# The output projection by seven products over halves, with branch a merged ahead of branch b

## The chip, the cores and the metric

One core of a Trainium2 chip runs the whole kernel. The metric is device microseconds from launch to end; lower is better. The kernel before took 1390.63 us, the median of 3 runs (1389.96 to 1392.5).

## The reference

One layer over 512 tokens of 2048 channels, all in float32:

```python
h = rmsnorm(x, norm_pre) * (1 + scale) + shift          # shift, scale, gate from c @ w_ada
q_a, f_a, v_a, z_a, v_b, z_b, g_a, g_b = split(h @ w_in)
y_a = hgrn2(q_a, f_a, v_a) / rms * hgrn_norm * silu(z_a)        # gated recurrence, 1024 wide
y_b = pool_mixer(v_b, pool_w, pool_scale) * silu(z_b)           # trailing windows, 1024 wide
merged = sigmoid(g_a) * (y_a @ w_proj_a) + sigmoid(g_b) * (y_b @ w_proj_b)
out = merged @ w_out                                            # 512 x 2048 by 2048 x 2048
return x + gate * rmsnorm(out, norm_post)
```

## The kernel before

Every large product is made of three: each operand is split into a high half that TensorE's fast float32 form holds exactly and the rest (`hi`, `lo`), and hi·hi, hi·lo and lo·hi are summed in PSUM. For weights this is `w_piece` (L156): one load on the sync queue into a `raw` tile, a copy to `hi` on ACT (L162) and the remainder `lo = raw - hi` on DVE, or on POOL where an engine is named or heads are being worked on (L163). `raw`, `whi` and `wlo` have four tiles each, so up to four pieces are under way. `split` (L166) does the same for activations. `load` (L66) fixes the order of the loads, `matmul` (L83) that of the products.

The stages follow each other: norm and modulation of x; the first part of the input projection while h comes in; the rest of it with the recurrence's steps between its products; the two gates g_a and g_b, whose sigmoids stay in SBUF as 32 tiles `sig[b][m]` (L726). Both branches' y have been put into DRAM before (`y_dram`) and are loaded and split again (L731 to L735). Then, for each pair m of 128-channel tiles, branch a's projection (48 products into `pa`), branch b's (48 into `pb`), the two gate products on DVE (L744, L745), their sum (L747) and its split into `mh`, `ml` (L748). Channels are on partitions, tokens along the free axis. TensorE takes the products in the order of the program, from L691 on; the other engines' order comes from a scheduler, which takes the earliest instruction of the program that it holds ready.

The output projection, `out_cols` (L755), has tokens on partitions. For each of four blocks of 512 columns four PSUM tiles are filled, one for a token tile, over 16 k-tiles with three products each:

```python
matmul(outs[t], mh[k][:, sl], w[0][:, r], k == 0, False)
matmul(outs[t], mh[k][:, sl], w[1][:, r], False, False)
matmul(outs[t], ml[k][:, sl], w[0][:, r], False, k == KT - 1)
```

A piece of weights is 2 k-tiles by 512 columns (L766), 24 products. In the last block the second half of the k-tiles goes token tile by token tile, so that a tile is done every 24 products. A done tile is squared and summed on ACT (L778), multiplied by the gate's row on DVE (L780); `finish` (L783) makes 1/rms in small steps on DVE with one square root on ACT, then scales four 512-wide parts and adds x, one part on POOL (L790, L791) and three on DVE (L793), and stores them. x is loaded again on POOL's queue while the last blocks run (L801).

Of the kernel before, what the change touches and what calls it, by code (L numbers as in the profile page):

```python
# [15 lines left out]
P = 128  # L16
D = 2048
S = 512
# [16 lines left out]
def trunk(ctx, tc, x, c, w_ada, b_ada, norm_pre, norm_post, w_in, lower_bounds, hgrn_norm,  # L35
# [4 lines left out]

    const = ctx.enter_context(tc.tile_pool(name="const", bufs=1))
    act = ctx.enter_context(tc.tile_pool(name="act", bufs=1))
    ring = ctx.enter_context(tc.tile_pool(name="ring", bufs=1))
    small = ctx.enter_context(tc.tile_pool(name="small", bufs=2))
# [3 lines left out]

    def t_h(name, dt=F32R):
        return act.tile([P, S], dt, tag="h", bufs=32, name=name)  # L50

    def t_s(name, dt=F32):
        return act.tile([P, S], dt, tag="s", bufs=32, name=name)

    def t_w(name, n=S, dt=F32):
        return act.tile([P, 528], dt, tag="w", bufs=10, name=name)[:, :n]
# [9 lines left out]
    def load(dst, src):  # L66
        """A load on the sync queue, issued in the order of these calls."""
# [15 lines left out]
    def matmul(o, lhsT, rhs, start, stop):  # L83
        """A product; with in_order set, TensorE issues them in the order of these calls."""
        if in_order[0] and last_mm[0] is not None:
            with tc.issue_after(last_mm[0]):
                d = nc.tensor.matmul(o, lhsT, rhs, start=start, stop=stop)  # L87
        else:
            d = nc.tensor.matmul(o, lhsT, rhs, start=start, stop=stop)  # L89
        last_mm[0] = ins_of(d)  # L90
# [5 lines left out]
    # the recurrence's heads, taken in steps between the products of the projections  # L96
# [25 lines left out]
    scan_mask = const.tile([P, S], F32, name="scan_mask")  # L122
    nc.vector.memset(scan_mask, 1.0)
    nc.vector.memset(scan_mask.rearrange("p (c t) -> p c t", t=CH)[:, :, 0:1], 0.0)
    inv_pos = const.tile([P, 16], F32, name="inv_pos")
# [3 lines left out]
    def band_mask(name, step, lo, hi, m, nb):  # L129
        """1 where step * b + lo <= s <= step * b + hi, for column (b, r), r < m."""  # L130
        t = const.tile([P, nb * m], F32, name=name)
# [8 lines left out]
    # masks[m][i][s, t']: s in the i-th quarter of the 4m-block whose later quarters hold t'  # L140
    masks = {m: [band_mask(f"mask_{m}_{i}", 4 * m, i * m, i * m + m - 1, (3 - i) * m, P // (4 * m)) for i in range(3)]
             for m in (2, 8)}
    mask_pair = const.tile([P, P], F32, name="mask_pair")
# [12 lines left out]
    def w_piece(name, src, k0, nk, c0, n, eng=None):  # L156
        """hi and lo halves, exact, of a block of weights: [P, nk, n] each."""
# [28 lines left out]
    # lower bound: softmax over the layers, its running sum less the first layer's  # L186
# [16 lines left out]
    def ada_sum(k, k0, n, src):  # L203
        """Two sums, over the even and the odd row tiles."""
# [11 lines left out]
    def ada(k0, nk, rows=range(KT)):  # L216
        """shift and scale for the k-tiles k0..: the products of c with w_ada, summed over its row tiles."""
        n = 2 * nk * P
        for k in rows:
            a = (t_h(f"ada_{k0}_{k}", F32) if k0 < 4 else t_s(f"ada_{k0}_{k}"))[:, :n]  # L220
# [16 lines left out]
    def rstd_of(ssum, n, tag, r):  # L237
        """r = 1 / sqrt(ssum / n + eps), [P, 1], with one Newton step."""
# [10 lines left out]
    # the scale's share without c: (1 + its bias) * norm_pre  # L249
# [6 lines left out]
    diag = [const.tile([P, P], F32, name=f"diag_{t}") for t in range(TT)]  # L256
# [48 lines left out]
    def cols(name, src, k0, nk, c0, xh, xl, outs, k_first, k_last, eng=None):  # L305
        """128 * len(outs) columns, channels on partitions, over the k-tiles k0.. of a sum k_first..k_last."""
# [29 lines left out]
    def v_half(i):  # L336
        """v for four heads, tokens on partitions."""
# [18 lines left out]
    y_dram = [dram.tile([NH, P, S], F32, name="ya_dram"), dram.tile([NH, P, S], F32, name="yb_dram")]  # L356
    sz_a = [None] * NH
# [397 lines left out]
    def out_cols(j, split_k, done):  # L755
# [11 lines left out]
        for k in range(0, split_k, 2):  # L767
            w = piece(k)
            for t in range(TT):
                for r in range(2):  # L770
                    mm(t, k + r, r, w)
# [60 lines left out]
```

## Time and profile before

| what | value |
|---|---|
| median of 3 runs | 1390.63 us (1389.96 to 1392.5) |
| span of the profiled execution | 1388.9 us |
| busy: PE, DVE, ACT, POOL | 1333.3, 777.2, 521.1, 265.2 us |
| mean granted TensorE clock | 0.990 |
| DRAM read, written | 182.51 MB, 8.39 MB |

The profile gives the span from the first to the last instruction of one execution; the time of that execution itself is not listed apart, and the median of the runs is 1.7 us above the span. Products are pipelined: the duration of one (389 ns) overlaps the next, so their cost is read from the distance of their starts, or from a long link of the chain of waits. [...]

### The profile page before, as it was taken

The page shows a single profiled execution, that of the slowest core. Times are in us where ns is not written, and L with a number is a line of the kernel's source. Part 1 is how long each engine was busy: PE and PEld are TensorE (multiplying, and loading weights), DVE is VectorE, ACT ScalarE, POOL GpSimd, SP SyncE. Part 2 cuts the span into 40 slices and gives each one's busy share as a digit, 9 for nine tenths or more (in the row PEclk, how much of TensorE's full clock was granted, in tenths as well). Part 3 has the DMA queues.
Part 4 walks back from the last instruction along what each step waited for, and adds up shares of the span by engine and source line. Part 5 has one row for each costly group of instructions (what it writes and reads, how often), then busy time and mean ns, then how long its engine had stood idle before and what let it go on. Part 6 is the DMA issues. An engine that isn't in the chain of part 4 may idle for free.

```text
span 1388.9 us, 16351 instructions
## 1 busy us (share of the span) xinstructions
PE 1333.3 (96%) x6105; PEld 1106.5 (80%) x6105; DVE 777.2 (56%) x1237; ACT 521.1 (38%) x745; POOL 265.2 (19%) x273
## 2 busy tenths in 40 slices
PE   2988899999999999999999999999999999999996
PEld 1777788888888888788888888888888888888885
DVE  6996854337668696786834445343254454432326
ACT  5543263353535645465542222222252222221221
POOL 3646451213321332222300000000010000200003
PEclk9999999999999999999999999999999999999999
DMA  9988633322131323323235545554352323623213
GB/s 334 326 291 280 192 110 123 97 84 87 42 129 61 114 76 103 102 73 125 92 119 170 194 146 190 163 179 153 127 167 93 106 91 100 218 92 106 91 61 122
DMA packets 160695, 191.97 MB, mean 138 GB/s; under 512 B 8460, under 2 KB 128356, under 8 KB 160616
## 3 DMA queue, kind: packets, MB, share of 16 engines
q1 hardware_dynamic: 156616, 178.30, 39.2%
q0 software_dynamic: 3840, 12.59, 2.6%
q8 instruction: 48, 0.79, 0.2%
q14 instruction: 31, 0.25, 0.1%
q10 hardware_dynamic: 160, 0.05, 0.0%
HBM read 182.51 MB, written 8.39 MB: 137 GB/s over the span
## 4 chain that ended last, share of the span: by engine, by line
PE 89%; DVE 4%; issue 2%; DMA 2%; POOL 1%; ACT 1%; SPq 0%; DVEq 0%; ACTq 0%; POOLq 0%
PE g_ps L87 25%; PE out L87 11%; PE g L89 7%; PE vb_ps L87 6%; PE za_ps L87 6%; PE v_ps L87 6%; PE pb L87 6%; PE pa L87 6%; PE zb_ps L87 5%; PE q_ps L87 3%; PE lv L87 2%; PE o L87 1%; DVE og L793 1%; DMA x<-in_x_dram 1%; PE mix L87 1%
## 5 line engine op out<-in xcount | busy, mean ns | idle before, releaser
L87 PE MATMUL g_ps<-h_hi,g_hi 128*128 128x512 f32 x512 | 200.5, 392 | 0.0
L87 PE MATMUL g_ps<-h_hi,g_lo 128*128 128x512 f32 x512 | 199.5, 390 | 0.0
L87 PE MATMUL g_ps<-h_lo,g_hi 128*128 128x512 f32 x512 | 199.5, 390 | 0.0
L162 ACT CAST g_hi<-g_raw 128x1024 fp32r<-128x1024 f32 x64 | 67.3, 1053 | 194.8 <-PE g_ps L87 164.1
L163 DVE TENSOR_TENSOR g_lo<-g_raw,g_hi 128x1024 fp32r<-128x1024 f32 x61 | 74.5, 1222 | 107.0 <-ACT g_hi L162 107.0
L87 PEld LDWEIGHTS g_ps<-h_lo,g_hi 128*128 128x128 f32 x512 | 96.4, 188 | 20.1
L87 PEld LDWEIGHTS g_ps<-h_hi,g_hi 128*128 128x128 f32 x512 | 96.4, 188 | 20.0
L87 PEld LDWEIGHTS g_ps<-h_hi,g_lo 128*128 128x128 f32 x512 | 96.3, 188 | 20.1
L211 DVE SCALAR_TENSOR_TENSOR ada_acc<-ada,c_act,ada_acc 128x512 f32<-128x512 f32 (+1 forms) x126 | 105.7, 902 | 0.0
L163 DVE TENSOR_TENSOR wo_lo<-wo_raw,wo_hi 128x1024 fp32r<-128x1024 f32 x32 | 39.2, 1225 | 111.2 <-ACT wo_hi L162 111.2
L87 PE MATMUL out<-wo_hi,m_hi 128*128 128x512 f32 x256 | 99.6, 389 | 0.0
L87 PE MATMUL out<-wo_lo,m_hi 128*128 128x512 f32 x256 | 99.6, 389 | 0.0
L87 PE MATMUL out<-wo_hi,m_lo 128*128 128x512 f32 x256 | 99.6, 389 | 0.0
L162 ACT CAST wo_hi<-wo_raw 128x1024 fp32r<-128x1024 f32 x32 | 33.7, 1053 | 119.3 <-PE out L87 106.9
L608 DVE SCALAR_TENSOR_TENSOR gate<-gw,c_act,gate 128x512 f32<-128x512 f32 x60 | 45.1, 751 | 45.2 <-DMA gw<-in_w_ada_dram 43.8
L734 POOL DMA_DIRECT2D y<-ya_dram x8 | 4.4, 550 | 288.2 <-DMA npost<-in_norm_post_dram 231.2
L87 PEld LDWEIGHTS out<-wo_hi,m_lo 128*128 128x128 f32 x256 | 48.0, 188 | 10.1
L87 PEld LDWEIGHTS out<-wo_lo,m_hi 128*128 128x128 f32 x256 | 48.0, 188 | 10.0
L87 PEld LDWEIGHTS out<-wo_hi,m_hi 128*128 128x128 f32 x256 | 48.0, 188 | 9.9
L87 PE MATMUL vb_ps<-h_hi,vb_hi 128*128 128x512 f32 x128 | 51.5, 402 | 0.0
L87 PE MATMUL za_ps<-h_hi,za_hi 128*128 128x512 f32 x128 | 51.1, 399 | 0.0
L87 PE MATMUL zb_ps<-h_hi,zb_hi 128*128 128x512 f32 x128 | 50.9, 398 | 0.0
(307 smaller groups left out, 3150.0 us busy)
## 6 DMA issues: line engine op xcount, KB each, us to landing
g_raw<-in_w_in_dram SPq DMA_DIRECT2D x64, 512.0 KB, 3.5
ada<-in_w_ada_dram SPq DMA_DIRECT2D x120, 256.0 KB, 5.1
gw<-in_w_ada_dram SPq DMA_DIRECT2D x64, 256.0 KB, 5.2
wo_raw<-in_w_out_dram SPq DMA_DIRECT2D x32, 512.0 KB, 3.6
v_raw<-in_w_in_dram SPq DMA_DIRECT2D x16, 512.0 KB, 3.7
vb_raw<-in_w_in_dram SPq DMA_DIRECT2D x16, 512.0 KB, 3.3
zb_raw<-in_w_in_dram SPq DMA_DIRECT2D x16, 512.0 KB, 3.4
za_raw<-in_w_in_dram SPq DMA_DIRECT2D x16, 512.0 KB, 3.5
```

What stands on the lines that cost most here:

```text
L87: d = nc.tensor.matmul(o, lhsT, rhs, start=start, stop=stop)
L89: d = nc.tensor.matmul(o, lhsT, rhs, start=start, stop=stop)
L162: last_w[0] = ins_of(nc.scalar.copy(hi, raw))
L163: (eng or (nc.gpsimd if steps and next(turn) else nc.vector)).tensor_sub(lo, raw, hi.bitcast(F32))
L211: nc.vector.scalar_tensor_tensor(acc, src, c_act[:, k:k + 1], acc, op0=ALU.mult, op1=ALU.add)
L608: nc.vector.scalar_tensor_tensor(gate[j], t, c_act[:, k:k + 1], gate[j], op0=ALU.mult, op1=ALU.add)
L734: nc.gpsimd.dma_start(y, y_dram[b][k])
L793: nc.vector.scalar_tensor_tensor(og[t][j], og[t][j], ro, xr[t][j], op0=ALU.mult, op1=ALU.add)
```

## The change

The 512 tokens, the k-tiles and the columns are halved for the output projection: tokens 0 to 255 and 256 to 511 (`lower`, `upper`), even and odd k-tiles of a pair (`me`, `mo`), and 512 columns beside 512 (`c` = 0, 1). With seven products of sums and differences of halves, instead of eight, the four quarter results are made (Strassen's scheme). The sums of the activations are built once, as seven 256-wide blocks S1 to S7 of an operand tile for each of 8 pairs (`operands`), split in hi and lo; the sums of the weights are built for each piece as it is loaded (`piece_1`, `piece_2`). A block of 1024 columns is made in two passes over the 8 pairs: M1, M5 and M2 first, then M6, M7, M3 and M4, where M3 and M4 go on in the banks of M5 and M2.

So that the 14 operand tiles find room, the branches are taken apart: all of branch a first, its gated values put into DRAM; then branch b with the sums. The sigmoids of g_b and the gate's rows go by way of DRAM too. The pools that hold the tiles are opened and closed to match; `h`'s high halves and low halves have pools of their own, and the low halves' room takes branch a's y, the high halves' that of branch b. Comments are dropped, and `matmul` passes on a flag for banks that are gone on with. Cut to its core:

```diff
@@ gate_finish, sigmoids
+        nc.gpsimd.dma_start(gate_dram[j], acc)
...
                 nc.scalar.activation(sig[b][m + r], o2[r], AF.Sigmoid)
+                if b == 1:
+                    nc.gpsimd.dma_start(sig_dram[1][m + r], sig[b][m + r])
@@ both branches
+    ya = load_y(0, t_hb)
+    ha_scope.close()
...
+    yb = load_y(1, lambda name: yb_pool.tile([P, S], F32R, tag="yb", bufs=16, name=name))
     for m in range(0, KT, 2):
         pa = [t_ps(f"pa_{m}"), t_ps(f"pa_{m + 1}")]
-        proj2(f"pa{m}", w_proj_a, NH, m * P, yh[0], yl[0], pa)
+        proj2(f"pa{m}", w_proj_a, NH, m * P, *ya, pa)
+        for r in range(2):
+            nc.vector.tensor_mul(sig[0][m + r], pa[r], sig[0][m + r])
+            nc.gpsimd.dma_start(sig_dram[0][m + r], sig[0][m + r])
+    phase.close()
...
+    def operands(p, me, mo, x12, x56, x7, alloc):
...
+        nc.vector.tensor_add(v(x12), v(me), mo[:, upper].unsqueeze(1).to_broadcast([P, 2, H]))
+        nc.vector.tensor_add(x56[:, lower], me[:, lower], mo[:, lower])
+        nc.vector.tensor_sub(x56[:, upper], me[:, upper], me[:, lower])
+        nc.vector.tensor_sub(x7, mo[:, lower], mo[:, upper])
...
+        nc.scalar.copy(o(hi, S1, 2), x12)
+        nc.scalar.copy(o(hi, S5, 2), x56)
+        nc.scalar.copy(o(hi, S7), x7)
+        nc.scalar.activation(o(hi, S3), me[:, lower], AF.Copy, scale=-1.0)
+        nc.scalar.copy(o(hi, S4), mo[:, upper])
+        nc.vector.tensor_sub(o(lo, S1, 2), x12, o(f, S1, 2))
+        nc.vector.tensor_sub(o(lo, S5, 2), x56, o(f, S5, 2))
+        nc.vector.tensor_sub(o(lo, S7), x7, o(f, S7))
+        nc.vector.scalar_tensor_tensor(o(lo, S3), me[:, lower], -1.0, o(f, S3), op0=ALU.mult, op1=ALU.subtract)
+        nc.vector.tensor_sub(o(lo, S4), mo[:, upper], o(f, S4))
...
+    for p in range(NP):
+        m = 2 * p
+        sa, sb = [], []
+        for r in range(2):
+            for b, t in ((0, sa), (1, sb)):
+                t.append(mrg.tile([P, S], F32, tag="mrg", bufs=8, name=f"s{b}_{m + r}"))
+                nc.gpsimd.dma_start(t[r], sig_dram[b][m + r])
         pb = [t_pg(f"pb_{m}"), t_pg(f"pb_{m + 1}")]
+        for k0 in range(0, NH, 4):
+            cols(f"pb{m}_{k0}", w_proj_b, k0, 4, m * P, *yb, pb, 0, NH - 1, w_eng())
         for r in range(2):
+            nc.vector.tensor_mul(sb[r], pb[r], sb[r])
+            nc.gpsimd.tensor_add(sa[r], sb[r], sa[r])
...
+            operands(p, sa[0], sa[1], sb[0], sb[1], x7, op_tile)
@@ output projection
+    def piece_1(j, p):
...
+        load(raw[:, 0], w[:, 0, 0])
+        load(raw[:, 1], w[:, 1, 1])
...
+        nc.vector.tensor_add(s[:, 0], raw[:, 0], raw[:, 1])
+        b = hi_lo(f"w1b_{j}_{p}", raw, nc.vector)
+        d = hi_lo(f"w1s_{j}_{p}", s[:, 0:1], nc.gpsimd, 1)
...
+    def piece_2(j, p):
...
+        load(ra, w[:, 0])
+        load(rb, w[:, 1])
...
+        nc.gpsimd.tensor_sub(s, rb, ra)
+        d = hi_lo(f"w2d_{j}_{p}", s, nc.vector)
+        nc.vector.tensor_add(ra[:, 0], ra[:, 0], ra[:, 1])
+        nc.vector.tensor_add(rb[:, 0], rb[:, 0], rb[:, 1])
...
+        for i, r in enumerate((ra, rb)):
+            nc.scalar.copy(hi[:, i], r[:, 0])
+            nc.vector.tensor_sub(lo[:, i], r[:, 0], hi.bitcast(F32)[:, i])
...
+    def product(name, p, w, banks_, first, last, onto):
+
+        for i in range(2):
...
+            matmul(banks_[name][i], sh, w[name][0], first, False, onto)
+            matmul(banks_[name][i], sh, w[name][1], False, False, onto)
+            matmul(banks_[name][i], sl_, w[name][0], False, last, onto)
+
+    def group(piece, j, order, last_order, banks_, begun, done, then=None):
+
+        for p in range(NP - 2):
+            w = piece(j, p)
+            for name in order:
+                product(name, p, w, banks_, p == 0 and name not in begun, False, name in begun)
+            if then and then[0] == p:
+                then[1]()
+        w2 = [piece(j, p) for p in (NP - 2, NP - 1)]
+        for name in last_order:
+            for i in range(2):
+                product(name, NP - 2 + i, w2[i], banks_, False, i == 1, name in begun)
+            done(name)
...
+        group(piece_1, j, ("M1", "M5", "M2"), ("M1", "M5", "M2"), bk, (), done_1)
...
+                if name == "M3":
+                    og[lo_t][j + 1], og[hi_t][j + 1] = alloc(lo_t, 1), alloc(hi_t, 1)
+                    square(lo_t, j + 1, bank)
+                    nc.vector.tensor_add(og[hi_t][j + 1], y[i], bank)
+                    gated(lo_t, 1, bank)
...
+                elif name == "M6":
+                    nc.vector.tensor_add(og[hi_t][j + 1], og[hi_t][j + 1], bank)
+                    square(hi_t, j + 1, og[hi_t][j + 1])
+                    gated(hi_t, 1, og[hi_t][j + 1])
+                    if j == 2:
+                        finish(hi_t)
+                else:
+                    nc.vector.tensor_add(y[i], y[i], bank)
+                    square(lo_t, j, y[i])
+                    gated(lo_t, 0, y[i])
+                    if j == 2:
+                        finish(lo_t)
+
+        order = ("M6", "M7", "M3", "M4")
+        group(piece_2, j, order, ("M3", "M4", "M6", "M7"), bk, ("M3", "M4"), done_2,
+              (4, load_x) if j == 2 else None)
...
-        for j in range(4):
+        for j in (0, 1, 3, 2):
...
+    out_block(0, lambda t, c: t_og(f"og_{t}_{c}"))
+    out_block(2, lambda t, c: in_spare(f"og_{t}_{2 + c}"))
```

`done_1` copies M1 out on ACT and takes M5 and M2 from it on DVE (two instructions each). `load_x` loads x in 16 transfers on POOL's queue into operand tiles that are used up. `w_eng` gives the remainders of branch b's weights to DVE and POOL in turn.

## Rows read from the trace of the kernel before

**Rows 1.** The page: engines' busy time, and parts of its 40 slices

```profile
PE 1333.3 (96%) x6105; PEld 1106.5 (80%) x6105; DVE 777.2 (56%) x1237; ACT 521.1 (38%) x745; POOL 265.2 (19%) x273
...
PE   2988899999999999999999999999999999999996
...
PEclk9999999999999999999999999999999999999999
...
GB/s 334 326 291 280 192 110 123 97 84 87 42 129 61 114 76 103 102 73 125 92 119 170 194 146 190 163 179 153 127 167 93 106 91 100 218 92 106 91 61 122
```

**Rows 2.** The chain of waits from 1192 us on: start, us, engine, tile, count

```profile
1192.14 10.88 PE pb L87 x48
1203.02 157.77 PE out L87 x696
...
1382.40 1.67 DVE og L793
```

**Rows 3.** Output projection: groups by line, then its window (engines' busy time)

```profile
L87 PE MATMUL out<-wo_hi,m_hi 128*128 128x512 f32 x256 | 99.6, 389 | 0.0
...
L163 DVE TENSOR_TENSOR wo_lo<-wo_raw,wo_hi 128x1024 fp32r<-128x1024 f32 x32 | 39.2, 1225 | 111.2 <-ACT wo_hi L162 111.2
...
L162 ACT CAST wo_hi<-wo_raw 128x1024 fp32r<-128x1024 f32 x32 | 33.7, 1053 | 119.3 <-PE out L87 106.9 <-PE pa L87 7.6 <-PE pb L87 4.8
...
1203.00:1377.10 174.10, 174.10 (x769) 143.82 (x767) 59.38 (x75) 42.98 (x64) 8.76 (x8) 1.00 0.29 102
```

**Rows 4.** The timeline of POOL and of DVE, 515 to 521 us, and POOL at 584

```profile
515.92 2.43 POOL L163 TENSOR_TENSOR vb_lo<-vb_raw,vb_hi 128x1024 fp32r<-128x1024 f32 x1
...
520.05 3.14 POOL L163 TENSOR_TENSOR zb_lo<-zb_raw,zb_hi 128x1024 fp32r<-128x1024 f32 x1
...
517.32 1.33 DVE L485 TENSOR_TENSOR Y<-R,G 128x256 f32<-128x256 f32 x1
518.57 0.41 DVE L485 TENSOR_TENSOR Y<-A,G 128x256 f32<-128x256 f32 x1
518.90 0.28 DVE L485 TENSOR_TENSOR X<-R,G 128x128 f32<-128x128 f32 x1
...
519.71 1.21 DVE L163 TENSOR_TENSOR vb_lo<-vb_raw,vb_hi 128x1024 fp32r<-128x1024 f32 x1
520.84 0.27 DVE L504 COPY sd<-lv 32x128 f32<-32x128 f32 x1
...
584.20 2.39 POOL L163 TENSOR_TENSOR za_lo<-za_raw,za_hi 128x1024 fp32r<-128x1024 f32 x1 [4.30 <-ACT za_hi L162]
```

**Rows 5.** The timeline of DVE and of POOL behind the last product

```profile
1378.45 0.68 DVE L780 TENSOR_TENSOR og<-out,gate 128x512 f32<-128x512 f32 x1
1379.05 0.14 DVE L785 TENSOR_REDUCE s<-ss 128x1 f32<-128x4 f32 x1
...
1380.55 3.52 DVE L793 SCALAR_TENSOR_TENSOR og<-og,ro,xr 128x512 f32<-128x512 f32 x3
...
1380.62 1.25 POOL L790 TENSOR_SCALAR og<-og,ro 128x512 f32<-128x512 f32 x1 [2.64 <-DVE ro L247]
1381.95 1.57 POOL L791 TENSOR_TENSOR og<-og,xr 128x512 f32<-128x512 f32 x1
...
L793 DVE SCALAR_TENSOR_TENSOR og<-og,ro,xr x12: 750/1183/1784, 1363.9 to 1382.3; 128x512 f32<-128x512 f32 x12
```

**Rows 6.** Single lines (ns min/median/max) and the list of DMA issues (us to landing)

```profile
L169 POOL TENSOR_TENSOR h_lo<-hf,h_hi x16: 1282/1513/5147, 29.6 to 184.3; 128x512 fp32r<-128x512 f32 x16
...
L801 POOL DMA_DIRECT2D xr<-in_x_dram x16: 548/548/548, 1191.5 to 1203.6; - x16
...
wo_raw<-in_w_out_dram SPq DMA_DIRECT2D x32, 512.0 KB, 3.6
```

**Rows 7.** Two windows around a pause of PE: engines' busy time, granted clock

```profile
562.80:565.40 2.60, 0.62 (x3) 0.23 (x2) 2.53 (x7) 1.25 (x2) 0.00 (x0) 1.00 0.60 195
566.40:569.70 3.30, 3.30 (x9) 2.62 (x8) 3.30 (x17) 2.86 (x4) 0.34 (x1) 0.50 0.01 2
```

More of the change, by code (lines that the diff above doesn't have):

```diff
@@ L255, in trunk @@
     rx = const.tile([P, TT], F32, name="rx")
-    diag = [const.tile([P, P], F32, name=f"diag_{t}") for t in range(TT)]
+    diag = [tables.tile([P, P], F32, name=f"diag_{t}") for t in range(TT)]
     with tc.high_priority():
@@ L751, in trunk @@
+        if p < NP - 1:
+            operands(p, sa[0], sa[1], sb[0], sb[1], x7, op_tile)
+    yb_scope.close()
+    last_op = ctx.enter_context(tc.tile_pool(name="last_op", bufs=1, side="right", reuse_waits="tile"))
+    operands(NP - 1, sa[0], sa[1], sb[0], sb[1], x7,
+             lambda name, dt: last_op.tile([P, 7 * H], dt, tag="last_op", bufs=2, name=name))
+    merge.close()
+    fin = ctx.enter_context(tc.tile_pool(name="fin", bufs=1, reuse_waits="tile"))
     og = [[None] * 4 for _ in range(TT)]
@@ new lines, in trunk, with t_og, ring_tile, w_rows @@
+    gate_sb = []
+    for j in range(4):
+        gate_sb.append(fin.tile([P, S], F32, tag="gate", bufs=4, name=f"gate_sb_{j}"))
+        nc.gpsimd.dma_start(gate_sb[j], gate_dram[j])
+    def t_og(name):
+        return fin.tile([P, S], F32, tag="og", bufs=10, name=name)
+    def ring_tile(tag, name, dt=F32R):
+        return ring.tile([P, 2, S], dt, tag=tag, bufs=4, name=name)
+    def w_rows(j, p):
+        return w_out[2 * p * P:(2 * p + 2) * P, j * S:(j + 2) * S].rearrange("(k p) (c n) -> p k c n", p=P, n=S)
@@ L794, in finish, with in_spare, load_x @@
             nc.sync.dma_start(out[t * P:(t + 1) * P, j * S:(j + 1) * S], og[t][j])
-    for j in range(3):
-        out_cols(j, KT, lambda t: None)
-    for t in range(TT):
-        for j in range(4):
-            xr[t][j] = t_h(f"xr_{t}_{j}", F32)
-            nc.gpsimd.dma_start(xr[t][j], x[t * P:(t + 1) * P, j * S:(j + 1) * S])
-    out_cols(3, KT // 2, finish)
+    spare = []
+    def in_spare(name):
+        if not spare:
+            t = op_tile(f"spare_{name}", F32)
+            spare.extend(t[:, i * S:(i + 1) * S] for i in range(3))
+        return spare.pop(0)
+    def load_x():
+        for t in (2, 3, 0, 1):
+            for j in range(4):
+                xr[t][j] = in_spare(f"xr_{t}_{j}")
+                nc.gpsimd.dma_start(xr[t][j], x[t * P:(t + 1) * P, j * S:(j + 1) * S])
+    out_block(0, lambda t, c: t_og(f"og_{t}_{c}"))
+    out_block(2, lambda t, c: in_spare(f"og_{t}_{2 + c}"))
 _INS = ["x", "c", "w_ada", "b_ada", "norm_pre", "norm_post", "w_in", "lower_bounds", "hgrn_norm",
```

144 lines of the change are left out of this document (96 added, 48 removed).

## The prediction

> **What bounds the kernel now.** I read the page first. TensorE (PE) is busy 1333.3 of the 1388.9 us, and from the sixth slice on every slice but the last is 90% busy or more, at the whole clock [rows 1]. The chain of waits says the same of the part that changes: each 48 products of a branch projection take 10.88 us, and 696 products of the output projection stand in one unbroken link of 157.77 us [rows 2]. That is 0.2267 us a product. The window of the output projection confirms it: PE is busy through all 174.1 us, DVE for 59.4, ACT for 43.0, POOL for 8.8 [rows 3]. So before the change only the number of products counts there, and the others have room. Behind the last product (1203.0 + 174.1 = 1377.1) stands a tail that belongs to DVE: its last instruction ends at 1384.1, and the stores and the end of the program take 4.8 us more [rows 2, 5].
>
> The span of the profiled execution is 1388.9 us and the median of the runs 1390.6. I add changes to the median and take the 1.7 us between as lying outside the span and unchanged. About 0.2% (2.8 us) is what a measurement of this kernel can tell from no change.
>
> **Products removed.** Before, there are 16 k-tiles x 4 token tiles x 4 column blocks x 3 = 768 products. After, each of 2 column pairs and 8 k-pairs has 7 products of halves x 2 token tiles x 3 = 42, together 672, of the same 128x512 shape. The 96 that go are worth 96 x 0.2267 = **-21.8 us**, since nothing hides PE there. The branch projections keep their 768 products; only their order changes.
>
> **Weights of the second half of a block.** An output block runs `group` twice. In the first pass (M1, M5, M2) a piece has 18 products, 4.08 us. Its weights ask of DVE one 512-wide sum and one 1024-wide remainder, of POOL one 512-wide remainder: 0.60 + 1.13 on DVE (start to start [rows 4, 5]) and 1.28 on POOL, the shortest of its 512-wide ones [rows 6]. Even end to end that is 3.0 of 4.08, so it is hidden. In the second pass (M6, M7, M3, M4) a piece has 24 products, 5.44 us. `piece_2` asks POOL for a 1024-wide difference (2.39 us [rows 4]) and DVE for a 1024-wide remainder, two 512-wide sums and two 512-wide remainders: 1.13 + 4 x 0.60 = 3.53 us. Each alone fits in 5.44; end to end they are 5.92.
>
> Do they run end to end? When POOL's remainder of 515.92 was running, DVE's 256-wide product of 517.32 took 1.33 us; the next of its kind took 0.41. It ended 0.3 us after POOL's. In turn POOL's remainder of 520.05 took 3.14 us instead of 2.39, longer by about what DVE's 1024-wide remainder still had to run [rows 4]. All of these read two operands from SBUF. I therefore take it that such a DVE instruction and a POOL one exclude each other. The rows hold few such meetings, and between two streams that meet rarely this cost little.
>
> The Trainium skill's page "SBUF — State Buffer", section "Who interferes with whom", states that a DVE instruction with two SBUF inputs and a GpSimd one that reads SBUF exclude each other for the whole instruction. By it the sum is the one below; by reading the rows as an occasional delay, the term of this part would be about 1 us, which is the first rival.
>
> At 5.92 us a piece the second pass is slower than its products. The first piece is ready in time, because the first pass gives the tiles of M1 back 5.44 us before its end. The second has its loads, difference and sums ahead, but takes the tiles of M2, which come free only at the end: 1.05 us of ACT [rows 3], then remainders of 1.13 and 1.2 and two evictions of M2 (1.2), about 5.0 us into the pass, 0.4 us ahead of its need. The loads give no more lead: with four raw tiles there are two pieces, and from a tile's release to the next one is landing 3.6 [rows 6] + 0.6 + 2.39 + 1.2 + 1.13 + 1.2 = 10.1 us, near the 10.88 of two pieces. So six pieces at 5.92 end at 40.5; the remainder of the last one's differences stands 2.4 us ahead of that, at 38.1. The closing order wants it for M3 after 6 x 5.44 + 1.36 = 34.0 us. PE waits 4.1 us, twice: **+8.2** (bounds 1 and 14; the upper end takes every landing late by 2 to 3 us, as x is loaded in the last pass, with 16 issues of 0.55 us on POOL [rows 6], 8.8 us ahead of or between its differences).
>
> **The tail.** Before, a token tile is finished every 5.44 us of products, so one finish stands behind the last product. After, the closing order completes M3, M4, M6, M7 at 2.72 us from each other, and all four token tiles are finished from M6 on. From 2.7 us before the last product ends, DVE has four sums and four gate products (8 x 0.60) and four finishes, each the small steps (1379.05 to 1380.55, 1.50 us, of which 0.6 wait on ACT and can be filled by another finish) and three wide steps that meet POOL's two (3.52 us for three instead of 3 x 0.67 [rows 5]): 4.8 + 4 x (0.9 + 3.53) - 2.7 = 19.8 us behind the last product, against 7.0 before: **+12.8**. Bounds: 6.7 more than before if POOL's two did not hold DVE up at all (4 x 2.9 + 4.8 - 2.7 = 13.7), 15.2 more if the small steps don't overlap either.
>
> **The seams**: from branch b to the first pass, between the passes, and to the second block. M1 is the first product asked for, and its weights go through DVE, ACT and POOL behind the last operands; at the second block M2 wants banks that DVE empties after M7. Nothing of before shows this seam. Its nearest row is the seam from branch b to the output projection, without a gap [rows 2]; the other bound is the chain of one piece, 0.6 + 0.6 + 1.3, at each of three. I take **+2** (0 to 7.5).
>
> **The clock.** Where PE stood idle for 2 of 2.6 us at 562.8, the granted clock was 0.5 for the stretch from 566.4 [rows 7], the level of 1.2 GHz; 3.3 us at half rate cost 1.7 us. Two waits of 4 us are new; I count one: **+1.7** (0 to 7).
>
> **At nothing.** Branch a ahead of b: POOL issues 72 more transfers (32 writes and 32 reads of the gated values, 4 and 4 of the last gate's rows) at 0.55 us each [rows 6]; the writes stand in stretches where POOL has little else, the reads are 4 in each 10.88 us of branch b. The branch weights are converted four pieces (21.8 us) ahead of their use, and that covers late sums and reads; without this cover a late gate value would show at once. Building the operands of a pair asks, with one weight piece on each engine, 1.13 + 3 x 0.60 + 6 x 0.33 = 4.9 us of DVE's work on two SBUF operands and 2.39 + 2 x 1.28 = 4.95 of POOL's in each 10.88: end to end it fits, with a tenth to spare. The first operands are used 87 us after branch a began, the last pair some 24 us after it can be begun. The DRAM traffic of branch b doubles to some 193 GB/s, below the 334 GB/s that the first slice moved [rows 1]. The pools of the input projection get other names and the same order of reuse.
>
> Sum: -21.8 + 8.2 + 12.8 + 2 + 1.7 = +2.9, **1393.5 us**.
>
> **Rivals.** (1) *The weights keep pace*: DVE and POOL meet rarely, the loads land early, PE never waits over 1 us in a pass and the clock holds. For it: each engine alone needs 3.5 and 2.4 of 5.44 us, and POOL was mostly idle here. Against it: the collisions, and a load-to-load chain as long as two pieces. -21.8 + 1 + 12.8 + 1 = -7.0: 1383.6, and 1380 with a tail between its bounds. (2) *Branch b falls behind*: the place is the loop that builds the operands, where DVE and POOL together hold 9.9 of 10.88 us; it decides once a meeting costs more than 1 us a round in lost time. At 1.9 us a round it is 1 us over, 8 rounds make 8 us, which surfaces at the first seam: 2.9 + 8 = +10.9, 1401.5; with the upper bounds of passes and clock some 1408. For it: waits there hold up whatever is queued behind on DVE, the next weights and the emptying of banks. Against it: the four pieces of lead. (3) That the change does not remove the products is excluded by the count.
>
> **How the numbers follow.** The forecast has 0.47, rival 1 has 0.34, rival 2 has 0.19. The forecast's own range is 1387.5 to 1400; of its share 0.01 lies below 1387.8, 0.19 within 0.2% and 0.27 above 1393.4. Rival 1 gives 0.32 faster and 0.02 the same, rival 2 all slower. Faster 0.33, same 0.21, slower 0.46. The range goes from 1380 (rival 1 with a shorter tail) to 1407.
>
> **What would show it.** Right: products `M...` at 0.2267 us apart in the first passes; in the second passes PE idle some 4 us in all, released by the remainders of `w2d` or `w2s`; POOL's difference at over 2.4 us and DVE's 512-wide sums at over 0.69 us mean; DVE's last wide step some 20 us behind the last product. Wrong: no idle of PE in the second passes (rival 1), branch b rounds over 10.88 us (rival 2), a tail under 14 us, or a part before branch a that is not the same.

## The result, and the profile after

The changed kernel takes 1444.45 us (median of 4 runs, 1441.31 to 1447.45) against 1390.91 us before: a ratio of 1.0386, 95% interval 1.0366 to 1.0406. It is slower by 53.5 us, far outside the predicted range. The profiled execution spans 1445.8 us against 1388.9.

The page of the changed kernel; its rows answer to [rows 1].

```profile
PE 1351.3 (93%) x6009; PEld 1092.5 (76%) x6009; DVE 865.5 (60%) x1373; ACT 557.6 (39%) x821; POOL 405.3 (28%) x401
...
PE   2899899999999999999999999999999999899973
...
PEclk9999999999999999999999999999999999899987
```

TensorE has 96 products fewer and is yet busy for 18 us more. The granted clock is no longer whole in the last slices. Four windows of the changed kernel, cut at branch b's last product and at the last of the seven products (times, engines' busy time, granted clock, DMA share, GB/s; the third answers to the window of [rows 3]):

```profile
1203.00:1227.60 24.60, 24.56 (x106) 19.43 (x104) 14.73 (x26) 7.07 (x13) 11.22 (x11) 1.00 0.36 120
1227.60:1234.90 7.30, 0.00 (x0) 0.00 (x0) 5.80 (x12) 2.59 (x6) 3.35 (x5) 0.78 0.18 50
1234.90:1421.70 186.80, 167.28 (x672) 131.76 (x672) 126.52 (x147) 70.50 (x110) 71.36 (x48) 0.94 0.44 150
1421.70:1445.80 24.10, 0.01 (x1) 0.00 (x0) 18.65 (x40) 3.32 (x9) 11.24 (x8) 0.60 0.47 174
```

They account for the 56.9 us of span. Branch b ends at 1227.6 instead of 1203.0: 24.6 us. TensorE then stands still for 7.3. The 672 products take 186.8 us where 768 took 174.1: 12.7. The tail has 24.1 instead of 11.8: 12.3. The largest single part of the loss lies *ahead* of the output projection, in a part whose instructions the change hardly touches.

The chain of waits of the changed kernel (start, us, what) shows where. Ahead of the output projection a run of wide products takes 14.70 / 63 = 0.2333 us each, where it was 10.88 / 48 = 0.2267 [rows 2]. Further down stands one turn of a second pass:

```profile
604.77 14.70 PE za_ps L102 x63
...
1292.76 4.40 DMA w2b<-in_w_out_dram
...
1297.32 2.40 POOL w2s L882
...
1299.74 0.69 DVE w2a L884
1300.43 0.60 DVE w2b L885
1301.03 0.86 DVE w2d_lo L859
...
1302.09 3.50 DVE w2s_lo L889 x2
1305.60 4.65 DMA w2b<-in_w_out_dram
```

That is a closed loop: a load, GpSimd's difference, VectorE's sums and low halves, and only then the next load into the same raw tile. One turn takes 1305.60 - 1292.76 = 12.84 us and makes two pieces, whose products need 10.88. The two low halves last 3.50 us because the first of them stands beside GpSimd's difference for the next piece, and the difference too takes 2.98 us instead of 2.40:

```profile
1301.44 2.98 POOL L882 TENSOR_TENSOR w2s<-w2b,w2a 128x1024 f32<-128x1024 f32 x1 [1.74 <-DMA w2b<-in_w_out_dram]
...
1302.09 2.88 DVE L889 TENSOR_TENSOR w2s_lo<-w2a,w2s_hi 128x512 fp32r<-128x512 f32 x1
```

What TensorE waited for from 1220 to 1425 us, in the changed kernel (us, times, longest):

```profile
PE m L102 <- DVE w2s_lo L889: 11.5, 5, 5.2
PE m L102 <- ACT w1s_hi L858: 7.4, 1, 7.4
PE m L102 <- POOL w1s_lo L859: 2.0, 3, 0.7
PE m L102 <- ACT w2d_hi L858: 2.0, 1, 2.0
PE m L102 <- ACT w2s_hi L888: 2.0, 2, 1.3
PE m L102 <- DVE w2d_lo L859: 1.8, 2, 0.9
```

### The profile page after: what moved, and what is told of

Its sections match the earlier page's. It is cut to its first block, busy times and chain, and to the rows that moved or that the text cites. A ratio compares the mean times of both kernels' runs of the same rounds, so it can differ in the third digit from the quotient of the medians.

```text
span 1445.8 us, 16755 instructions
## 1 busy us (share of the span) xinstructions
PE 1351.3 (93%) x6009; PEld 1092.5 (76%) x6009; DVE 865.5 (60%) x1373; ACT 557.6 (39%) x821; POOL 405.3 (28%) x401
## 4 chain that ended last, share of the span: by engine, by line
PE 63%; issue 15%; DVE 9%; POOL 7%; DMA 5%; ACT 1%; SPq 0%; POOLq 0%; DVEq 0%; ACTq 0%
PE g_ps L102 24%; PE za_ps L102 6%; PE vb_ps L102 6%; PE v_ps L102 6%; PE zb_ps L102 5%; PE m L102 4%; PE g L104 3%; PE q_ps L102 3%; DMA w2b<-in_w_out_dram 3%; PE lv L102 2%; POOL w2s L882 2%; POOL s L825 1%; DVE ada_acc L226 1%; PE o L102 1%; DVE w2s_lo L889 1%
## 5 line engine op out<-in xcount | busy, mean ns | idle before, releaser
L747 POOL DMA_DIRECT2D sb_dram<-sig x16 | 8.7, 542 | 173.5 <-ACT sig L745 173.5
L882 POOL TENSOR_TENSOR w2s<-w2b,w2a 128x1024 f32<-128x1024 f32 x16 | 39.6, 2476 | 60.2 <-DMA w2b<-in_w_out_dram 59.1
L102 PE MATMUL pb<-y_hi,pb_hi 128*128 128x512 f32 x128 | 50.6, 396 | 0.0
L102 PE MATMUL pb<-y_hi,pb_lo 128*128 128x512 f32 x128 | 50.6, 395 | 0.0
L102 PE MATMUL pb<-y_lo,pb_hi 128*128 128x512 f32 x128 | 50.6, 395 | 0.0
L102 PE MATMUL zb_ps<-h_lo,zb_hi 128*128 128x512 f32 x128 | 50.6, 395 | 0.0
L102 PE MATMUL vb_ps<-h_hi,vb_lo 128*128 128x512 f32 x128 | 50.6, 395 | 0.0
L102 PE MATMUL za_ps<-h_lo,za_hi 128*128 128x512 f32 x128 | 50.6, 395 | 0.0
L102 PE MATMUL vb_ps<-h_lo,vb_hi 128*128 128x512 f32 x128 | 50.6, 395 | 0.0
```

Of the source, the lines that this page charges most:

```text
L102: d = nc.tensor.matmul(o, lhsT, rhs, start=start, stop=stop, skip_group_check=onto)
L747: nc.gpsimd.dma_start(sig_dram[1][m + r], sig[b][m + r])
L882: nc.gpsimd.tensor_sub(s, rb, ra)
```

## The experiments

All times are medians; ratios are to the kernel before in the same runs. "Realigned" is explained in the first experiment, and the repairs after it stand on it.

| kernel | us | ratio (95%) |
|---|---|---|
| changed | 1444.45 | 1.0386 (1.0366 to 1.0406) |
| realigned | 1424.51 | 1.0242 (1.0222 to 1.0262) |
| before, all pools 192 B on | 1389.45 | 0.9998 (0.9989 to 1.0008) |
| before, all pools 128 / 256 B on | 1389.39 / 1389.05 | one run each |
| before, ring alone 192 B on | 1403.53 | 1.0096 (1.0079 to 1.0112) |
| before, ring alone 64 / 128 / 256 B on | 1413.42 / 1415.26 / 1392.5 | one run each |
| realigned, sums at raised priority | 1422.1 | 1.0231 (1.0201 to 1.0261) |
| realigned, differences on VectorE | 1404.04 | 1.0101 (1.0057 to 1.0145) |
| realigned, sums in their own tile | 1414.09 | 1.0173 (1.0135 to 1.0212) |
| realigned, closing steps on VectorE | 1417.42 | 1.0197 (1.0156 to 1.0239) |
| realigned, first sums ahead | 1418.77 | 1.0202 (1.0179 to 1.0224) |
| four repairs | 1388.92 | 0.9988 (0.9974 to 1.0002) |
| and no GpSimd arithmetic | 1389.12 | 0.9990 (0.9977 to 1.0004) |
| and last operand later | 1387.51 | 0.9986 (0.9966 to 1.0006) |
| and x behind the weights | 1384.76 | 0.9955 (0.9936 to 0.9974) |

### The slower products: where the tiles lie

A product has two operands: one, 128 columns wide, is loaded into TensorE by an instruction of its own (PEld; it is called stationary here), the other, 512 columns wide, belongs to the product's instruction (it is called moving). In the built program of before, the activations' tiles, the ring of weights and the output projection's operands all begin at 256 modulo 512 bytes of a partition. In the changed one the ring and the seven products' operands still do (but for those of the last pair), while the activations begin at 448 and branch b's at 480, since the new pools are packed in another order. The first experiment adds two small pads that bring the activations back to 256:

```diff
+    pad_l = phase.enter_context(tc.tile_pool(name="pad_l", bufs=1)).tile([P, 80], F32, name="pad_l")
...
+    pad_r = ctx.enter_context(tc.tile_pool(name="pad_r", bufs=1, side="right")).tile([P, 56], F32, name="pad_r")
```

> The changed kernel with 320 bytes of unused space ahead of the pools of the input projection and 224 bytes at the other end, so that h and both branches' y start, as in the kernel before, at an even multiple of 256 bytes of a partition and not 192 beside one. Theory (the place of an operand sets the pitch of the products): the 4608 products ahead of the output projection go from 0.2333 us back to 0.2267 us each, 30 us less, about 1414 us; waits of the output projection and the tail stay. Rival (the traffic by way of DRAM, the longer program or its semaphores slow the products): pitch stays at 0.2333, 1444 us.

Measured: 20 us of the loss go, two thirds of the 30 expected. The chain of waits of the realigned kernel has the old pitch, 12.24 / 54 = 0.2267:

```profile
599.88 12.24 PE za_ps L104 x54
```

Branch b ends at 1204.0, 1.0 us later than before the change. From the first product of v to branch b's last one the realigned kernel takes 997.8 us and the one before 997.7; the changed one took 1018.5, 20.8 more than before. The expectation had counted the same delay for all 4608 products; those of v have a smaller one (below), and the rest of the difference was not traced. The 7.4 us of gap, the products (186.9 us) and the tail (24.1) stay as they were. So the pads cure the pitch and nothing else.

Is it the place itself? The kernel before, with a pad ahead of both the activations and the ring, moves all of them together by 192, 128 or 256 bytes:

```diff
+    pad = ctx.enter_context(tc.tile_pool(name="pad", bufs=1)).tile([P, 48], F32, name="pad")
...
     act = ctx.enter_context(tc.tile_pool(name="act", bufs=1))
```

> The kernel before with 192 bytes of unused space ahead of its two large pools; nothing else is changed. Theory (place of the operands): pitch 0.2333 or more in all 5376 wide products, so 36 us more or above, 1426 us or slower. Rival (something else of the change slows the products): 1390 us as before.

> The same with 128 bytes. If only multiples of 256 are fast: some 1426 us; if multiples of 128 do: 1390 us. The rival again 1390 us.

> The same with 256 bytes. If multiples of 256 are enough: 1390 us, pitch 0.2267; if multiples of 512 are faster still: pitch below 0.2267, and below 1380 us. The rival 1390 us.

Measured: nothing moved. The place by itself does not count. What is left is the distance between the two operands of a product. With the pad between the activations' pool and the ring, only that distance changes:

```diff
     act = ctx.enter_context(tc.tile_pool(name="act", bufs=1))
+    pad = ctx.enter_context(tc.tile_pool(name="pad", bufs=1)).tile([P, 48], F32, name="pad")
...
     ring = ctx.enter_context(tc.tile_pool(name="ring", bufs=1))
```

> The kernel before with 192 bytes of unused space between the pool of activations and the ring of weights: of each wide product one operand stays and the other is 192 bytes on, as in the changed kernel. Theory (the distance of the two operands' places sets the pitch): 0.2333 us instead of 0.2267, 5376 products, 36 us more, 1426 us. Rival (what slowed the changed kernel was the place of h alone or something else of the change): 1390 us.

> The same with 64 bytes. Theory: the distance is again no multiple of 256, pitch above 0.2267; were only the order of the two within 256 bytes to count, another value than with 192. Rival: 1390 us.

> The same with 128 bytes. If the distance counts in steps of 128 it is as before, 1390 us; if in steps of 256, slower like 192, 1426 us.

> The same with 256 bytes. If the distance counts in steps of 256: 1390 us; if in steps of 512: another pitch, above or below 0.2267.

Measured: distance it is. The times stay under the 1426 us expected, in part because not every distance costs the same; the rest was not traced. The chains of waits, a branch projection (activations move, the ring's weights are stationary) and the output projection (the other way round). With the ring 192 bytes on:

```profile
1035.30 10.99 PE pa L89 x48
...
1211.08 162.41 PE out L89 x696
```

With the ring 64 bytes on:

```profile
1045.11 11.20 PE pa L89 x48
...
1224.31 159.33 PE out L89 x696
```

With the ring 128 bytes on, and then 256:

```profile
1045.23 11.16 PE pa L89 x48
```

```profile
1030.89 10.88 PE pa L89 x48
```

Per product, by the start of the moving operand less that of the stationary one, modulo 256 bytes: at 0 it takes 0.2267 us (10.88 / 48), at 64 it takes 0.2289 (10.99 / 48 and 159.33 / 696), at 128 it takes 0.2324 (66.92 / 288, from the start of the projection shown to that of the sixth behind it at 1112.15 us), at 192 it takes 0.2333 (11.20 / 48 and 162.41 / 696). The same step of 64 or 192 bytes gives the other value where the operands change roles, so it is their difference with its sign. The changed kernel's activations lie 448 - 256 = 192 bytes on: 0.2333, as its chain showed. In its products of v the weights move, so that the distance is 64 there, and its chain has 43.96 / 192 = 0.2290:

```profile
209.06 43.96 PE v_ps L102 x192
```

Why the distance acts so was not tried.

### The seam

On VectorE the sum of the first weight piece stands right behind the last operand's low halves, in the changed kernel's timeline:

```profile
1233.15 0.42 DVE L804 TENSOR_TENSOR op_lo<-s,op_hi 128x256 fp32r<-128x256 f32 x1
1233.48 1.29 DVE L869 TENSOR_TENSOR w1s<-w 128x512 f32<-128x512 f32 x2
```

The first attempt raises the priority of the first two pieces.

```diff
+            with tc.high_priority() if piece is piece_1 and j == 0 and p < 2 else nullcontext():
-            w = piece(j, p)
+                w = piece(j, p)
```

> The changed kernel with its tiles realigned (1424.5 us) and the first two products' weight sums of branch a taken at high priority, so that VectorE and GpSimd make them ahead of the last operand of branch b. Theory (the 7.4 us of TensorE idle at the seam is the order of VectorE's work, sum behind operand): the gap between branch b's last product and the first of the seven products falls from 7.4 to under 2 us, the half clock behind it goes, and the time falls by 7 to 10 us, to about 1416. Rival (the operands of the seven products themselves come too late, or the sums now delay branch b's last operands): the idle time is found again within 20 us of the seam, and the time stays within 2 us of 1424.5.

Measured: 1422.1 us, which the intervals don't tell from the realigned 1424.5, and the wait is as it was:

```profile
PE m L104 <- ACT w1s_hi L862: 7.4, 1, 7.4
```

The two first sums still stood behind the last operand (the first starts at 1209.0 us, 5.9 behind branch b's last product); the sum's tile also lies over branch b's activations, which its last products read. Which of the two holds the sum up was not tried apart. So the second attempt gives the first passes' sums a small pool of their own and makes the first two pieces ahead of the last merge steps:

```diff
+    early = ctx.enter_context(tc.tile_pool(name="early", bufs=1, reuse_waits="tile"))
...
-        s = fin.tile([P, 2, S], F32, tag="sum", bufs=2, name=f"w1s_{j}_{p}")
+        s = early.tile([P, 1, S], F32, tag="early", bufs=2, name=f"w1s_{j}_{p}")
...
+        if p == NP - 1:
+            ahead.update({(0, q): piece_1(0, q) for q in range(2)})
```

> The realigned kernel (1424.5 us) with the sums of the first two weight pieces in a small pool of their own and made before the last operand of the merge. In the kernel with raised priority the gap of 7.37 us stayed to the hundredth, and the sum's tile lies over tiles that branch b's last products and the last operands still read. Theory (the place of the sum's tile and its place in VectorE's order make it wait, 7.4 us and the half clock behind it): the gap falls under 1 us, the half clock of 6.8 to 10 us behind it (3.4 to 5 us of lost work) goes, time falls by 8 to 12 us to 1413 to 1417. Rival (the high half's ring, freed by branch b's last product, or ScalarE, holds the first piece anyway): a gap of 2 us or more stays at the seam and under 6 us are gained.

Measured: the gap of 7.4 us is gone, but only 5.7 us of time. TensorE's waits from 1195 to 1400 us in this kernel, the three largest:

```profile
PE m L104 <- DVE w2d_lo L830: 6.8, 4, 3.0
PE m L104 <- POOL w1s_lo L830: 6.6, 5, 2.8
PE m L104 <- DVE w2s_lo L900: 6.5, 4, 2.3
```

The products begin right behind branch b, but their window grows from 186.9 to 191.5 us, so that only 2.8 of the 7.4 us are left; the rest of the gain lies ahead of the seam, where branch b's last product ends at 1200.25 us instead of 1204.01. All waits but the gap add up to 22.8 us (23.1 in the realigned kernel): those for GpSimd's low half have grown from 2.0 to 6.6, the longest of them, 2.8, for the third piece; those of the second passes have fallen from 21.1 to 15.6. And TensorE is busy for 168.6 us with the same products instead of 163.8, at a mean granted clock of 0.93 instead of 0.94. Why they share out so was not tried.

### The second passes

Two experiments cut the loop in two places. One puts GpSimd's difference on VectorE:

```diff
-        nc.gpsimd.tensor_sub(s, rb, ra)
+        nc.vector.tensor_sub(s, rb, ra)
```

> The realigned kernel with the differences of the second passes (16 of 2.4 us on GpSimd) put on VectorE beside the sums and the low halves. Theory (the second passes wait for a chain in which GpSimd's difference stands and holds up VectorE's low halves, 2.9 us where they take 1.2 alone): a VectorE difference of two 128x1024 tiles takes about 1.2 us, VectorE then works for 4.7 us of each 5.4, the waits of TensorE in the second passes fall from about 21 us to under 10, and the time by 10 to 15 us, to about 1411. Rival (the landing of the raw weights sets the pace: 4.4 to 4.7 us for two tiles, up to 10 beside other loads): waits and time unchanged within 4 us, and the wait rows name the load.

Measured: 20.5 us faster. The window of the products, and the groups of the difference and the low halves; first this kernel's, then those of the realigned one:

```profile
1211.10:1380.10 169.00, 160.63 (x672) 128.77 (x672) 131.95 (x163) 70.51 (x110) 32.80 (x32) 0.97 0.50 166
...
L886 DVE TENSOR_TENSOR w2s<-w2b,w2a 128x1024 f32<-128x1024 f32 x16 | 19.6, 1224 | 19.2 <-DMA w2b<-in_w_out_dram 14.7 <-POOL w1s_lo L863 4.5
L863 DVE TENSOR_TENSOR w2d_lo<-w2s,w2d_hi 128x1024 fp32r<-128x1024 f32 x16 | 19.5, 1219 | 0.0
...
L893 DVE TENSOR_TENSOR w2s_lo<-w2a,w2s_hi 128x512 fp32r<-128x512 f32 x16 | 11.0, 685 | 0.0
```

```profile
L886 POOL TENSOR_TENSOR w2s<-w2b,w2a 128x1024 f32<-128x1024 f32 x16 | 39.7, 2482 | 60.8 <-DMA w2b<-in_w_out_dram 57.1 <-DVE y L937 2.0 <-DVE w2b L889 1.5
...
L863 DVE TENSOR_TENSOR w2d_lo<-w2s,w2d_hi 128x1024 fp32r<-128x1024 f32 x16 | 22.6, 1413 | 0.0
...
L893 DVE TENSOR_TENSOR w2s_lo<-w2a,w2s_hi 128x512 fp32r<-128x512 f32 x16 | 15.2, 951 | 0.0
```

The difference takes 1224 ns instead of 2482, and VectorE's low halves, of the difference and of the first sum, fall from 1413 and 951 ns to 1219 and 685. VectorE got more work and did it sooner. The products' window shrinks from 186.9 to 169.0 us. The other experiment writes the sums to a tile of their own, so that the raw tiles come free sooner:

```diff
-        nc.vector.tensor_add(ra[:, 0], ra[:, 0], ra[:, 1])
+        s2 = fin.tile([P, 2, S], F32, tag="sum2", bufs=1, name=f"w2t_{j}_{p}")
+        nc.vector.tensor_add(s2[:, 0], ra[:, 0], ra[:, 1])
...
```

> The realigned kernel with the sums of the second passes written to a tile of their own in place of back over the raw weights, so that the raw tiles come free as soon as difference and sums have read them, about 3 us sooner. Theory (the ring of raw tiles bounds the second passes: the next load is issued only once the low half of the sum is made): the loads are issued 2.5 to 3 us sooner, the period of a pass step falls from 13 towards 10.9 us and the time by 5 to 12 us, to 1412 to 1419. Rival (the lock between VectorE and GpSimd, or the chain of the operations themselves, bounds them): the loads start sooner, TensorE's waits stay, time within 3 us of 1424.5.

Measured: 10.4 us faster with every instruction still there. GpSimd's idle time before its differences that ends with a load falls from 57.1 us in the realigned kernel to 31.9:

```profile
L886 POOL TENSOR_TENSOR w2s<-w2b,w2a 128x1024 f32<-128x1024 f32 x16 | 42.4, 2650 | 41.2 <-DMA w2b<-in_w_out_dram 31.9 <-DVE w2d_lo L863 4.5 <-DVE w2t L889 4.4
```

So both are true: the ring of raw tiles bounded the passes, and GpSimd's difference cost its loop time twice: by its own 2.48 us, where VectorE needs 1.22, and by holding VectorE's low halves up.

### The tail

```diff
-            if j == 0:
+            if j < 0:
                 nc.gpsimd.tensor_scalar(og[t][j], og[t][j], ro, 1.0, op0=ALU.mult, op1=ALU.mult)
```

> The realigned kernel with the closing steps of the last columns all on VectorE and none on GpSimd. Theory (the 12.3 us that the tail grew are VectorE's wide steps behind the last product, each stretched where GpSimd works beside it): GpSimd's part was 3 of the steps' time and VectorE's steps go back to their lone duration; the tail falls from 24.1 to about 21 us and the time by 3 us. Rival (VectorE's own work is the sum that counts, so that what GpSimd took is added to it): the tail grows by 1 to 4 us.

Measured: 7.1 us faster, of which the tail gives 4.7; the rest, within the interval, has no place in the profile. Its window, and VectorE's closing step (ns min/median/max), which took up to 1746 ns in the changed kernel:

```profile
1398.40:1417.80 19.40, 0.00 (x0) 0.00 (x0) 15.56 (x44) 3.32 (x9) 0.00 (x0) 0.59 0.59 216
...
L987 DVE SCALAR_TENSOR_TENSOR og<-og,ro,spare_xr x6: 744/745/745, 1402.3 to 1412.3; 128x512 f32<-128x512 f32 x6
```

VectorE works through 15.56 of the 19.4 us that remain.

### All of it together

The four repairs in one kernel (the second version of the seam):

> All four repairs at once on the realigned kernel: first sums ahead of the last operand and in a pool of their own, differences of the second passes on VectorE, their sums in a tile of their own, all closing steps on VectorE. Theory (each cost stands apart: 20 us of GpSimd in the second passes, 7 to 10 of the seam, 5 of the tail, 2 to 5 of raw tiles released late, since their 10 alone overlaps the 20): 1424.5 - 20 - 9 - 5 - 3 = 1387, with 1383 to 1393, a ratio of 0.995 to 1.002 to the kernel before; what is then left of the seven products' saving is 21.8 less a tail that is still some 7 us longer, less some 5 to 8 of waits. Rival (the waits are VectorE's load and take each other's place, so the gains don't add): above 1396.

Measured: 1388.92 us, not to be told from before. Alone the repairs gave 20.5 + 10.4 + 5.7 + 7.1 = 43.7 us, together 35.6, so some 8 us were counted twice (each single gain is uncertain by 4 to 7 us). The products' window is 165.6 us. Next, GpSimd's last arithmetic leaves the output projection, and the closing mean square is made for two token tiles at once:

```diff
-        d = hi_lo(f"w1s_{j}_{p}", s[:, 0:1], nc.gpsimd, 1)
+        d = hi_lo(f"w1s_{j}_{p}", s[:, 0:1], nc.vector, 1)
...
```

> The four repairs (1388.9 us, the seven products' TensorE waits 8 us and a half clock of 6.8 us behind the largest of them) with GpSimd taken out of the output projection altogether: the low half of the first passes' sums (16 of 1.3 us, up to 3.3 where VectorE is at work) on VectorE, and the closing mean square made for two token tiles at once. Theory (what is left at the seam is the lock again: GpSimd's low half took 3.25 us where it takes 1.3 alone, and TensorE waited 2.8 us for it): the waits named after that low half, 4.1 us, fall under 1.5 us, the half clock at 1212 goes (3.4 us), the pairs give 1 to 2 us in the tail; 1380 to 1385, ratio 0.993 to 0.997. Rival (ScalarE's copies behind the last operand, not GpSimd, are what is late): the wait is named after another step of the same piece, and under 3 us are gained.

Measured: 1389.12 us, no gain in the median where 4 to 9 us were expected. In its profile the gap behind the seam is gone and the products take 162.5 us, but the pairs gave nothing: the tail is 19.4 us again. Then the last operand is made behind the third piece:

```diff
-        group(piece_1, j, ("M1", "M5", "M2"), ("M1", "M5", "M2"), bk, (), done_1)
+        group(piece_1, j, ("M1", "M5", "M2"), ("M1", "M5", "M2"), bk, (), done_1, (2, close_merge))
```

> As the kernel without GpSimd in the output projection, and the last operand of the merge is made behind the third weight piece, since its five low halves, its sums and five copies (some 4 us of VectorE and 2.7 us of ScalarE) stand ahead of that piece and the operand itself is wanted only some 24 us later. Theory: no wait over 0.5 us is left within 15 us of the seam, no half clock there; 1379 to 1384, at most 3 us under the kernel without this step, ratio 0.991 to 0.996. Rival (the fourth piece is now late behind the operand): the gap comes back some 8 us later and the time is that of the kernel without it.

Measured: 1387.51 us, no difference that can be told. Two waits were left, named in the next expectation. For them, x is loaded behind the weights on their own queue, and the second block's first piece is made during the closing steps of the first:

```diff
+            halves = [piece_2a(j, p) for p in (NP - 2, NP - 1)]
+            if j == 2:
+                load_x()
+            w2 = [piece_2b(j, NP - 2 + i, *halves[i]) for i in range(2)]
...
+            if piece is piece_2 and j == 0 and name == "M4":
+                ahead[2, 0] = piece_1(2, 0)
...
-                nc.gpsimd.dma_start(xr[t][j], x[t * P:(t + 1) * P, j * S:(j + 1) * S])
+                load(xr[t][j], x[t * P:(t + 1) * P, j * S:(j + 1) * S])
```

> As the last kernel (1387.5 us; in its output projection two waits are left, 2.6 us at the second block's first piece and 3.7 us in the last pass, each with a half clock behind it), with two changes: the 16 loads of x go on the weights' queue behind the last weights, no longer beside them, and the second block's first piece is made between M4's and M6's closing steps of the first, with the rings' tiles of the last two pieces taken in an order that frees them for it. Theory (the transfers of x hold up the weights' landing, and VectorE's closing steps of the first block hold up the first sum of the second): both waits fall under 1 us and both half clocks go: 2.6 + 3.7 + 1.7 + 3.4 = 11 us at most, 6 to 10 likely; 1378 to 1382, ratio 0.991 to 0.995. Rival (x now lands too late for the closing steps, or the tail grows by what leaves the passes): the tail is over 21 us, or the time within 3 us of 1387.5.

Measured: 1384.76 us, ratio 0.9955 (0.9936 to 0.9974): 5.8 us under the 1390.53 of the kernel before in the same runs, and not the 1378 to 1382 expected. The interval meets that of the kernel above (0.9966 to 1.0006), so the gain of this last step alone is not certain. Two windows of its profile, and the only wait of TensorE listed for them, at the second block's first piece, where it had been 2.6 us:

```profile
1200.95:1355.40 154.45, 152.95 (x673) 125.51 (x671) 138.97 (x186) 72.73 (x114) 5.09 (x6) 1.00 0.54 181
1355.40:1374.90 19.50, 0.00 (x0) 0.00 (x0) 14.56 (x35) 3.02 (x7) 0.00 (x0) 0.59 0.60 215
```

```profile
PE m L104 <- DVE w1s_lo L834: 1.5, 1, 1.5
```

The products need 154.45 us instead of 174.1, at 152.95 / 673 = 0.2273 us each and at the whole clock. With the longer tail the output projection is 185.9 - 173.95 = 12.0 us shorter. That is the profile of the shortest of ten executions (1376.67 us; the longest 1389.59), so the median shows less; over the ten the mean granted clock goes from 0.990 in this one down to 0.981. In the first 206 us, which the repairs leave alone, this profile has 728 products at a granted clock of 0.98, that of the kernel above 712 at 0.93. Why the clock differs so, and why the times spread more than in the kernel before (1389.08 to 1392.47 in these runs), was not tried.

## Why the prediction was wrong

- **"The pools of the input projection get other names and the same order of reuse": at nothing.** This step failed first, and it is the largest single miss. Branch b ended 24.6 us later; 20.8 of them lie between the first product of v and branch b's last one, and the pads alone took them back (20 us in the medians). The other 3.8 lie ahead of that, where profiles of realigned kernels differ by as much: v starts at 203.8 us in the one with first sums ahead and at 208.1 in the one with the last operand later (208.9 in the changed kernel). The order of reuse was indeed the same, but the start of the activations against the weights was not, and no row of before could show a distance that was 0 everywhere. "A part before branch a that is not the same" stood among the signs of a wrong prediction, and that is what came.
- **Products removed, -21.8.** Right: once nothing holds them up, 672 products take 154.45 us, 19.7 less than the 768.
- **Second passes, +8.2.** That they fall behind their products was right; what sets their pace, and the size, was not. TensorE was idle for 186.80 - 167.28 = 19.5 us in the products' window, 17.3 of them in the waits for `w2...`. The step that failed is the loop "from a tile's release to the next one landing", which I put at 10.1 us and under the 10.88 of two pieces. It took 12.84: the landing 4.40 to 4.65 for my 4.2, and the two low halves 3.50 for my 1.2. I had counted the collisions of VectorE and GpSimd into the sum of their work (5.92 us a piece) and left them out of the loop, where they fall on the path. In the last pass the loop was longer still, where loads beside those of x took 6.90 and 10.08 us to land. My upper bound of 14 would not have held it.
- **VectorE and GpSimd exclude each other.** Right, and the experiment on the difference shows it: with it gone from GpSimd the low halves fall from 1413 to 1219 ns and from 951 to 685. The Trainium skill's page "SBUF — State Buffer", section "Who interferes with whom", says that such a pair blocks for the whole instruction; these durations agree. Rival 1, in which the weights keep pace, is out.
- **The clock, +1.7.** Too small. I counted one wait; there were four stretches at half clock (0.50 granted, the level of 1.2 GHz; 10.2, 3.4, 6.8 and 6.8 us, the first begun in the gap at the seam). TensorE was busy for 167.28 us with products that take 672 x 0.2267 = 152.3 at the whole clock, 15.0 more: 9.1 of it in these stretches, where it was busy for 19.7 us with 47 products; the other 5.9 was not traced.
- **The seams, +2.** 7.4 us at the first, at the end of its bounds (0 to 7.5). I had priced the chain of one piece; ahead of it stood the whole of the last operand.
- **The tail, +12.8.** Right: 12.3, with GpSimd's two steps holding VectorE up as worked out (4.7 us went with them).
- **Branch a ahead of b, at nothing.** Right: realigned, branch b ends 1.0 us later than before, so rival 2 did not happen. The traffic was put at 193 GB/s; the realigned kernel moved 191 from 1125 to 1195 us.

By my terms, corrected: -21.8 + 19.5 + 15.0 + 7.3 + 12.3 + 24.6 = 56.9, the span's difference. Against the +2.9 forecast the misses are 24.6 for the pools, 11.3 for the waits, 13.3 for the clock and what goes with it and 5.3 for the seam, less 0.5 for the tail. So the pools are not the whole of it: with them put right the kernel still took 1424.5 us, above the 1407 at which my range ends.

## What to carry to other kernels

When a change re-lays the pools, compare the starts of moving and stationary operands modulo 256 bytes first: a difference slowed every product of 512 columns here by up to 3%, and no wait shows it. Where a ring that holds two pieces feeds a loop, add up the loop with the durations that its steps have beside each other, not alone; a step moved to a slower engine can cost twice. Saving TensorE's work makes everything around it the bound: here 96 products fewer, 21.8 us, gave 5.8 us in the median, and only after the tiles' places, the seam, the second passes, the tail and the loads of x had been put right.

## What was not expected of the hardware

The pitch of products with 512 columns depends on the distance of their operands' starts: 0.2267, 0.2289, 0.2324 and 0.2333 us at 0, 64, 128 and 192 bytes modulo 256. And one VectorE sum took 4.91 us where its kind takes 0.68. The changed kernel's timeline round it:

```profile
1375.71 2.67 POOL L999 DMA_DIRECT2D spare_xr<-in_x_dram  x5
...
1376.40 4.91 DVE L885 TENSOR_TENSOR w2b<-w2b 128x512 f32<-128x512 f32 x1
1378.39 2.35 POOL L882 TENSOR_TENSOR w2s<-w2b,w2a 128x1024 f32<-128x1024 f32 x1
```

It spans most of GpSimd's five issues of x and the whole of the difference behind them, and TensorE's longest wait in the products' window, 5.2 us, ended with the low half behind it. The realigned kernel's profile has it again, 4.91 us beside issues and a difference. Sums that met issues alone took 0.68 us (at 1383.57 and 1384.17 us in the changed kernel), so the issues by themselves don't explain it; the cause is open. A half clock followed (0.50, the level of 1.2 GHz), as it did with the waits of 7.4, 1.9 and 3.1 us in this kernel and not after one of 2.0 (granted clock in the last column but two):

```profile
1374.00:1381.90 7.90, 3.17 (x13) 2.06 (x11) 6.11 (x3) 2.13 (x4) 7.88 (x10) 1.00 0.61 205
1381.90:1388.70 6.80, 5.60 (x13) 4.44 (x14) 5.29 (x8) 2.18 (x4) 3.05 (x6) 0.50 0.91 278
```
